# A layer's output weights taken early into the place of a finished scan, one vector's matrix moved into the up loop, and two projections of a scan in another order

## The chip, the cores and the metric

The kernel runs on one core of a Trainium2 chip. The metric is the device time of one execution in microseconds (us). TensorE (PE in the profile) multiplies matrices into PSUM, VectorE (DVE) and ScalarE (ACT) work elementwise, GpSimd (POOL) helps VectorE, and SyncE (SP) issues all the weight transfers, one queue in order. Each engine runs its own instructions strictly in the order in which they stand in its program, so an instruction that waits holds up everything behind it on that engine.

## The reference

A two-layer network over 256 context tokens and 256 latent tokens (512 columns in all, width 1024), and then a second block. The part that the change touches is layer 0 (`even_mixer`, then `conv_ffn`) and the beginning of layer 1 (`odd_mixer`, the SSD scan):

```python
mod_l = silu(c) @ mod_w[layer] + mod_b[layer]      # six vectors per layer: (layer, 0..5)
hl = modulate(xl, norm_mix_g[layer], sh1l, sc1l)
# layer 0: a GLA scan (4 heads) and an mLSTM scan (4 heads) of projections of h
yc, yl = even_mixer(hc, hl, ...)                   # concat([gla, mlstm]) @ w_out
xl = xl + g1l * yl                                 # vector 2
hl = modulate(xl, norm_ffn_g[layer], sh2l, sc2l)   # vectors 3 and 4
xl = xl + g2l * conv_ffn(hl, ...)                  # vector 5: needed after the down product only
# layer 1: SSD; each of 4 groups projects x, B, C and the gate z from h
```

## The kernel before

Every fp32 weight block is loaded into a staging tile `st` (three of them, pool `wst`), split by ScalarE into a half-precision high part `whi` and by VectorE or GpSimd into a low part `wlo`, and used in three TensorE passes; `get_w` does the load and the split, and its `parts` names the pool of the two parts. A staging tile is free for the next load when its `wlo` has been made.

The order of the instructions on each engine is set by a scheduler that builds the program, from the order in the code and from which tiles are free. A pool that is closed gives its memory to pools opened later, and a tile in that memory waits until the old tiles there have had their last reader.

Layer 0's mixer (`layer0_mixer`) goes in these steps. First `gla`: the projections of q, k, v (`gqk`, `gv`), and then four units (`gla_unit`: two pairs of heads, two streams). A unit makes eight levels of tiles `R` (VectorE subtracts, ScalarE takes the exponential, VectorE multiplies; four buffers), small products of them on TensorE (`PA`, `PB`, `fine`), picks blocks of these by masks into `acc` and `PT` (VectorE), then the output product `o`, a norm (`hsq`, `hss`, `rsqrt`, `on`) and a transpose `yT`, which ScalarE copies to `yf`. Then `mlstm_inputs`: the projections `mqk` (8 blocks of 128 rows, 512 columns), `mv`, `mo` and `gg`, 14 weight blocks of 1 MB in layer 0 in all. Then `mlstm`: four heads, each with masks `plain` and `msk`, exponentials `W`, products `S` and `nd` and a normalised sum `hm`. Last the output projection `eo` with the four weight blocks `even_o`: blocks 0 and 1 need the GLA half only, 2 and 3 the mLSTM half. Its results are added to the residual stream `xT`, which is loaded again from memory at this point. The modulation vectors are made by `mod_steps`: (0,2), (0,3), (0,4) as whole fp32 products beside the mLSTM heads, (0,5) after the output projection; those of layer 1 in half-precision halves of 0.5 MB, one in each of the 22 rounds of the FFN's up loop and the rest in the down loop. In the code all of `mlstm_inputs` comes after `gla`, and the scheduler weaves the two together.

In the SSD (`ssd`), `inputs` projects for a group x (`sx`), B and C (`sB`, `sC`) and the gate (`sz`); `steps` computes the decay terms of all groups while group 0 is projected.

Of the kernel before, what the change touches and what calls it, by code (L numbers as in the profile page):

```python
# [248 lines left out]
class Program:  # L249
# [287 lines left out]

    def layer0_mixer(self):
        h, I = self.h, self.I
        with ExitStack() as ph:  # L540
            gp = self.pool("gp", 1, None, ph)
            ev = self.pool("ev", 1, None, ph)
            mp = self.pool("mp", 1, None, ph)
            yf = ev.tile([128, 8, 512], F32, name="yf")
            mqk = ev.tile([128, 8, 512], F32, name="mqk")
            vext = ev.tile([128, 4, 4, 129], F32, name="vext")
            self.rows = [mp.tile([128, 512], F32, name=n) for n in ("li", "lf", "lb", "lm")]
            for t in self.rows:
                self.G.memset(t[:64], 0.0)
            self.G.memset(vext[:, :, :, 128:129], 1.0)  # L550
            self.gla(gp, h, I["even_w"], yf)
            self.mlstm_inputs(h, I["even_w"], mqk, vext, yf)
            for i in range(4):
                self.split(h[0][:, i], h[1][:, i], yf[:, i])
            self.mlstm(mp, h, mqk, vext, yf)
            self.dbg("ym", h[0])
        self.res2 = self.pool("res2")
        self.xT = self.res2.tile([128, 8, 512], F32, name="xT")
        self.nc.sync.dma_start(self.xT, I["xT"].rearrange("p (k t) -> p k t", k=8))
        with ExitStack() as tail:  # L560
            tw = self.pool("tw", 2, None, tail)
            w = [self.get_w(I["even_o"][b], 4, 512) for b in range(2)]
            for r in (2, 3, 4):
                for _ in self.mod_steps(0, r, whole=True):
                    pass
            w += [self.get_w(I["even_o"][b], 4, 512, parts=tw) for b in (2, 3)]

            for b in range(2):
                for c in range(4):
                    ps = self.mm("eo")  # L570
                    self.proj_fm(ps, w[b], c * 128, 128, h, 0, 512, nk=4)
                    self.add_residual(ps, 0, 2, 4 * b + c, BOTH)

            for s in range(2):
                for b in range(2):
                    for c2 in range(2):
                        ps = self.mm("eo")
                        for c in range(2):
                            self.proj_fm(ps[:, c * 256:c * 256 + 256], w[2 + b], (2 * c2 + c) * 128, 128, h,
                                         256 * s, 256 * s + 256, nk=4, h0=4)  # L580
                        for c in range(2):
                            self.add_residual(ps[:, c * 256:], 0, 2, 4 * b + 2 * c2 + c, ((s, 0, 256),), 256 * s)
                if s == 0:
                    self.norm_stream(0, 1, 0, "ml")
            for _ in self.mod_steps(0, 5, pool=tw, whole=True):
                pass
        self.dbg("xmid0", self.xT)

    def conv3(self, u, ps, w, b, streams=((0, 256), (256, 512))):
# [383 lines left out]
    def ffn(self, l, streams):  # L973
        I, V = self.I, self.V
        both = len(streams) == 2
# [4 lines left out]
        if both:  # L980
# [3 lines left out]
            for i in range(3):  # L984
                w = self.get_w(I["w_up"][l, i], 8, 256, self.G)
# [21 lines left out]
        with ExitStack() as ph:  # L1007
            fp = self.pool("fp", 1, None, ph)
            f2 = self.pool("f2", 3, None, ph)
            stage = self.pool("stage", 1 if both else 3, None, ph)  # L1010
            fcw = fp.tile([128, 44, 9], F32, name="fcw")
            self.nc.sync.dma_start(fcw, I["fcw"][l].rearrange("p (c j) -> p c j", c=44))
            hid = self.pair(fp, "hid", [128, 22, n])
            if both:
                ms, mp = self.pool("ms", 3, None, ph), self.pool("mp", 3, None, ph)
                up = True
                mods = chain.from_iterable(self.mod_steps(1, r, eng=lambda: self.G if up else None, pool=ms, parts=mp,
                                                          halves=True) for r in range(6))
            for i in range(22):
                begun = both and i < 3  # L1020
                if begun:
                    w, pss = first[i]
                elif not both and i < 2:
                    w = self.first_up[i]
                else:
                    w = self.get_w(I["w_up"][l, i], 8, 256, self.G if both or i > 2 else None, (None, stage)[i % 2])
                us = []
                for c in range(2):
                    ps = pss[c] if begun else self.mm("up")
                    a = 256 if begun else 0  # L1030
                    self.proj_fm(ps[:, a:n], w, c * 128, 128, h, a, n)
                    u = f2.tile([128, n], F32, tag=f"u{c}", name="u")
                    conv(u, ps, 22 * c + i)
                    us.append(u)
                sg = f2.tile([128, n], F32, tag="sg", name="sg")
                self.act(sg[:, :n], us[1][:, :n], AF.Silu)
                self.tt(sg[:, :n], sg[:, :n], us[0][:, :n], ALU.mult, eng=self.G)
                self.split(hid[0][:, i], hid[1][:, i], sg[:, :n], eng=self.G)
                if both:
                    next(mods)  # L1040

            def down(k, ws, a, b):
                ps = self.mm("dn")
                for j, w in enumerate(ws):
                    self.proj_fm(ps[:, a:b], w, 0, 128, hid, a, b, nk=11, h0=11 * j, first=j == 0, last=j == 1)
                    for _ in range(3 - j if both else 0):
                        next(mods, None)
                return ps

            def weights(k, j, parts=None):  # L1050
                return self.get_w(I["w_dn"][l, 2 * k + j], 11, 128, self.G if not both and k < 2 else None, (None, stage)[j], parts)

            up = False
            if not both:
                self.ahead()
            for k in range(6 if both else 8):
                self.add_residual(down(k, [weights(k, j) for j in range(2)], 0, n), l, 5, k, streams, t0)
                if not both:
                    self.before_norm(k)
                    if k >= 4 and k < 4 + 3:  # L1060
                        for i in (0, 1):
                            self.first_mg.append(self.get_w(I["w2_m"][2 * (k - 4) + i], 8, 128, self.G, stage, self.nx, 2048, 1024))
            if both:

                ws = [[weights(k, j, fp if (k, j) == (7, 1) else None) for j in range(2)] for k in (6, 7)]
                for s, a, b in streams:
                    for k in (6, 7):
                        ps = down(k, ws[k - 6], a, b)
                        self.add_residual(ps[:, a:b], l, 5, k, ((s, 0, 256),), a)
                    if s == 0:  # L1070
                        self.norm_stream(1, 0, 0)
# [15 lines left out]
    def ssd(self, sp, s2, h, y):  # L1087
        T, V, I = self.T, self.V, self.I
# [107 lines left out]
        for b in range(2):  # L1196
            w = self.get_w(sw[b], 8, 256)
# [5 lines left out]
        def inputs(g, d):  # L1203
# [3 lines left out]
            for b in range(2):  # L1207
                if g:
                    w = self.get_w(sw[5 * g + b], 8, 256)
                else:  # L1210
                    w, pss = first[b]
# [12 lines left out]
                    yield  # L1224
            if g == 0:
                d["steps"] = steps(pd)
            w = self.get_w(sw[5 * g + 2], 8, 256)
            ps = self.mm("sB")
            self.proj_fm(ps, w, 0, 128, h, 0, 512)
# [15 lines left out]
            cb = d["cb"] = s2.tile([128, 2, 128], F32, tag="cb", name="cb")  # L1245
            self.act(cb, ps[:, :256].rearrange("p (a b) -> p a b", a=2))
            yield
            sz = d["sz"] = s2.tile([128, 4, 256], F32, tag="sz", name="sz")
            for b in range(2):
                w = self.get_w(sw[5 * g + 3 + b], 8, 256)  # L1250
# [115 lines left out]

        D = {}
        take(inputs(0, D), 99)
        states(0, D)
        for g in range(4):  # L1370
# [631 lines left out]
```

## Time and profile before

| | us |
|---|---|
| median of 3 runs (1649.72 to 1652.54) | 1651.38 |
| the profiled execution, its own time | 1646.42 |
| span of the profile, first to last instruction | 1644.6 |
| TensorE busy | 1563.6 |
| VectorE busy | 1212.3 |
| ScalarE busy | 847.9 |
| GpSimd busy | 444.8 |

The profile is of one execution; its own time is 1.8 us more than its span and 5 us less than the median. Times in the rows are microseconds from the start of the span. A busy share of 95% for TensorE says that in most stretches it is TensorE's queue that sets the pace; the stretches in which it isn't busy show where another engine or a transfer does.

### The profile page before, as it was taken

The numbers are of one execution on the slowest core, as the hardware profiler recorded it, in microseconds if no ns is written. First come the engines' busy times: TensorE is split into PE (matmuls) and PEld (weight loads), VectorE is DVE, ScalarE is ACT, GpSimd is POOL, SyncE is SP. The second block draws the span as 40 slices with busy tenths as digits, with TensorE's granted clock in tenths as the row PEclk, the third lists the DMA queues.
The fourth block names the chain that finished last, engine by engine and source line by source line (L and its number), as shares of the span: only waits on it lengthen the run. The fifth ranks groups of instructions, "written<-read, shape, count | busy, mean of one in ns | idle before, by whom it ended". The sixth has DMA issues, their size and how long they took to land.

```text
span 1644.6 us, 31809 instructions
## 1 busy us (share of the span) xinstructions
PE 1563.6 (95%) x12978; PEld 1083.6 (66%) x12978; DVE 1212.3 (74%) x2637; ACT 847.9 (52%) x1390; POOL 444.8 (27%) x264
## 2 busy tenths in 40 slices
PE   6999999889999999998999999699998999999998
PEld 3565875467444444475566667488887887778877
DVE  6888856777877796557878898799977885366734
ACT  4746434334555445435555665356564644566542
POOL 0000000224878740000000000259934312431250
PEclk9999999989999999999999999799999999999999
DMA  9222135752444437532222343335454343433651
GB/s 392 89 103 79 54 126 208 258 183 80 157 149 146 138 122 254 177 120 77 103 78 95 112 141 125 124 121 199 137 194 166 141 167 111 146 116 125 228 168 52
DMA packets 41187, 236.77 MB, mean 144 GB/s; under 512 B 4689, under 2 KB 5457, under 8 KB 21201
## 3 DMA queue, kind: packets, MB, share of 16 engines
q1 hardware_dynamic: 41040, 234.74, 40.6%
q8 instruction: 102, 1.67, 0.4%
q14 instruction: 45, 0.36, 0.1%
HBM read 233.68 MB, written 1.05 MB: 143 GB/s over the span
## 4 chain that ended last, share of the span: by engine, by line
PE 81%; DVE 8%; ACT 4%; DMA 3%; issue 3%; POOL 1%; ACTq 0%; SPq 0%; DVEq 0%; POOLq 0%
PE up L332 19%; PE dn L332 9%; PE sx L332 5%; PE fm L332 4%; PE mg L332 4%; PE br L332 3%; PE mqk L332 2%; PE tm L339 2%; ACT whi L306 2%; PE so L332 2%; DVE wlo L294 2%; PE mod L505 2%; PE sz L332 2%; DVE u L303 2%; PE sc L1664 2%
## 5 line engine op out<-in xcount | busy, mean ns | idle before, releaser
L332 PEld LDWEIGHTS <-whi 128*128 128x128 f16 (+2 forms) x5240 | 511.5, 99 | 253.3 <-issue 38.1
L294 POOL TENSOR_TENSOR wlo<-st,whi 128x2048 bf16<-128x2048 f32 (+2 forms) x101 | 311.7, 3097 | 935.5 <-ACT whi L306 934.8
L306 ACT ACTIVATE whi<-st 128x2048 f16<-128x2048 f32 (+3 forms) x242 | 369.1, 1536 | 253.3 <-PE dn L332 46.6
L332 PEld LDWEIGHTS <-wlo 128*128 128x128 bf16 (+2 forms) x2620 | 258.9, 99 | 127.4 <-issue 13.6
L294 DVE TENSOR_TENSOR wlo<-st,whi 128x2048 bf16<-128x2048 f32 (+4 forms) x141 | 279.0, 1988 | 83.8 <-ACT whi L306 82.1
L303 DVE SCALAR_TENSOR_TENSOR u<-up,fcw,u 128x189 f32<-128x189 f32 (+3 forms) x792 | 297.3, 431 | 49.4 <-ACT u L306 41.5
L332 PE MATMUL up<-hh,whi 128*128 128x256 f16 (+1 forms) x752 | 238.2, 319 | 4.4 <-ACT hh L306 4.1
L332 PE MATMUL up<-hl,whi 128*128 128x256 bf16 (+1 forms) x752 | 238.1, 317 | 2.0 <-DVE hl L303 1.9
L332 PE MATMUL up<-hh,wlo 128*128 128x256 f16 (+1 forms) x752 | 237.7, 317 | 0.0
L332 PE MATMUL dn<-hidh,wlo 128*128 128x256 f16 (+1 forms) x396 | 122.2, 310 | 2.3 <-DVE wlo L294 2.3
L332 PE MATMUL dn<-hidh,whi 128*128 128x256 f16 (+1 forms) x396 | 122.3, 311 | 1.8 <-ACT whi L306 1.8
L332 PE MATMUL dn<-hidl,whi 128*128 128x256 bf16 (+1 forms) x396 | 122.5, 310 | 0.0
L306 ACT ACTIVATE u<-up,ppt,fcw 128x512 f32<-128x512 f32 (+1 forms) x88 | 58.1, 660 | 47.9 <-PE up L332 47.9
L332 PE MATMUL fm<-hh,whi 128*128 128x256 f16 x288 | 78.5, 273 | 0.5 <-DVE xc L303 0.5
L332 PE MATMUL fm<-hh,wlo 128*128 128x256 f16 x288 | 78.6, 273 | 0.0
L332 PE MATMUL fm<-hl,whi 128*128 128x256 bf16 x288 | 78.5, 273 | 0.0
L332 PE MATMUL mg<-hh,wlo 128*128 128x256 f16 x256 | 71.0, 277 | 3.6 <-POOL wlo L294 3.6
L332 PE MATMUL mg<-hl,whi 128*128 128x256 bf16 x256 | 71.0, 278 | 1.2 <-DVE hl L303 1.2
L332 PE MATMUL mg<-hh,whi 128*128 128x256 f16 x256 | 70.7, 277 | 0.9 <-ACT mgt L306 0.9
L339 PEld LDWEIGHTS <-hh 128*128 128x128 f16 x640 | 61.5, 99 | 8.8 <-issue 1.1
L298 POOL TENSOR_SCALAR E<-E,rs 128x128 f32<-128x128 f32 (+1 forms) x48 | 37.1, 786 | 107.3 <-DVE rs L1675 47.9
L294 POOL TENSOR_TENSOR sg<-sg,u 128x512 f32<-128x512 f32 (+1 forms) x44 | 44.2, 1004 | 45.6 <-ACT sg L306 45.3
(539 smaller groups left out, 3050.8 us busy)
## 6 DMA issues: line engine op xcount, KB each, us to landing
st<-in_w_up_dram SPq DMA_DIRECT2D x44, 1024.0 KB, 4.8
st<-in_w_dram SPq DMA_DIRECT2D x25, 1024.0 KB, 4.9
st<-in_mod_w_dram SPq DMA_DIRECT2D x48, 512.0 KB, 4.7
st<-in_w_dn_dram SPq DMA_DIRECT2D x32, 704.0 KB, 4.1
st<-in_ssd_w_dram SPq DMA_DIRECT2D x20, 1024.0 KB, 4.9
st<-in_mod_w_dram SPq DMA_DIRECT2D x16, 1024.0 KB, 6.4
st<-in_w_m_dram SPq DMA_DIRECT2D x32, 512.0 KB, 4.3
st<-in_even_w_dram SPq DMA_DIRECT2D x14, 1024.0 KB, 5.0
```

The lines of the kernel that those rows point to most:

```text
L294: (eng or self.V).tensor_tensor(o, a, b, op=op)
L298: (eng or self.V).tensor_scalar(o, a, s1, None, op0=op0)
L303: self.V.scalar_tensor_tensor(o, a, s, b, op0=op0, op1=op1)
L306: self.S.activation(o, i, func, **kw)
L332: self.T.matmul(ps, w[a][:, k, c0:c0 + cw], h[b][:, h0 + k, t0:t1], start=first and k == 0 and i == 0, stop=last and k == nk - 1 and i == 2)
L339: self.T.matmul(ps, h[b][:, k, t0:t0 + 128], w[a][:, k, c0:c0 + cw], start=k == 0 and i == 0, stop=k == nk - 1 and i == 2)
L505: T.matmul(ps[32 * j:32 * j + 32, :256], c[:, 2 * b + k], w[:, 0 if halves else k, 256 * j:256 * j + 256], start=b == k == i == 0, stop=b ...
L1664: T.matmul(ps[:, a:b], q[r, tb * 128:tb * 128 + 128], k[r, 0:b - a], start=True, stop=False)
```

## The change

Four edits. The GLA tiles (`gp`) go to the right side of the memory and are closed when `gla` ends, and the four `even_o` blocks are fetched and split at that point, ahead of the mLSTM projections, their low parts on GpSimd and their parts in the place of the GLA tiles (`tw`, four buffers). The vector (0,5) is no longer made after the output projection, but in halves at the head of the chain that the up loop draws from, two halves in each of the first 8 rounds. The residual stream's tile is still opened after the mixer's left-hand pools are closed. In the SSD, group 0's gate projections come ahead of its B and C.

```diff
     def layer0_mixer(self):
         h, I = self.h, self.I
+        tail = self.ctx.enter_context(ExitStack())
         with ExitStack() as ph:
-            gp = self.pool("gp", 1, None, ph)
+            gs = ExitStack()
+            gp = self.pool("gp", 1, None, gs, side="right")
...
             self.gla(gp, h, I["even_w"], yf)
+
+            gs.close()
+            tw = self.pool("tw", 4, None, tail, side="right")
+            w = [self.get_w(I["even_o"][b], 4, 512, self.G, parts=tw) for b in range(4)]
             self.mlstm_inputs(h, I["even_w"], mqk, vext, yf)
...
-        with ExitStack() as tail:
-            tw = self.pool("tw", 2, None, tail)
-            w = [self.get_w(I["even_o"][b], 4, 512) for b in range(2)]
+        with tail:
             for r in (2, 3, 4):
...
-            w += [self.get_w(I["even_o"][b], 4, 512, parts=tw) for b in (2, 3)]
...
-            for _ in self.mod_steps(0, 5, pool=tw, whole=True):
-                pass
...
-                mods = chain.from_iterable(self.mod_steps(1, r, eng=lambda: self.G if up else None, pool=ms, parts=mp,
-                                                          halves=True) for r in range(6))
+                mods = chain.from_iterable(self.mod_steps(*m, eng=lambda: self.G if up else None, pool=ms, parts=mp,
+                                                          halves=True) for m in ((0, 5), *((1, r) for r in range(6))))
...
-                if both:
+                for _ in range(0 if not both else 2 if i < 8 else 1):
                     next(mods)
...
             if g == 0:
                 d["steps"] = steps(pd)
+                yield from gate(g, d)
...
+            if g:
+                yield from gate(g, d)
```

The change moves far more instructions than it edits. TensorE's program of the kernel before, where the GLA units begin: behind the first small products (`PA`, `fine`, `PB`) stand already the matmuls of `mqk`, the first mLSTM projection, and they alternate with GLA products from here on.

```order
L736 MATMUL PA<-R 128x256 x8
L802 MATMUL fine<-QK 32x32 x13
L780 MATMUL PB<-R 128x128 x2
L780 MATMUL PB<-R 64x64 x4
L802 MATMUL fine<-QK 32x32 x3
L332 LDWEIGHTS whi
L332 MATMUL mqk<-hh,whi 128x512
L332 LDWEIGHTS whi
L332 MATMUL mqk<-hl,whi 128x512
```

TensorE's program of the changed kernel, where the first `mqk` matmul stands now: right behind the last unit's `o` and `yT`.

```order
L832 MATMUL o<-gv,PC 128x128 x2
L838 MATMUL yT<-ept,on 128x128 x4
L332 LDWEIGHTS whi
L332 MATMUL mqk<-hh,whi 128x512
L332 LDWEIGHTS whi
L332 MATMUL mqk<-hl,whi 128x512
```

All products of the four GLA units stand ahead of the first projection of the mLSTM; before, only those of the first rows above did. Between the units there are only the masks `plain` and `msk` of three of the mLSTM's eight head directions.

ScalarE's program of the changed kernel at the same place (`yf` is the copy of a unit's output, `whi` a high part, `u` the evacuation of a projection):

```order
L306 ACTIVATE hsq<-o 128x512
L306 ACTIVATE yf<-yT,hglag 128x256 x2
L306 ACTIVATE whi<-st 128x2048 x7
L306 ACTIVATE u<-mqk,hcb,hcw 128x512
```

The seven high parts, four of `even_o` and then three of `mqk`, stand behind the last unit's copy; before, the high parts of the projections stood between the units' exponentials.

SyncE's queue before, from the small GLA load `a` on:

```order
L625 DMA a_517<-in_a_dram 128x512
L315 DMA st<-in_even_w_dram 128x2048 x9
L315 DMA st<-in_even_o_dram 128x2048 x2
L315 DMA st<-in_mod_w_dram 128x2048 x2
L559 DMA xT<-in_xT_dram 128x4096
L315 DMA st<-in_mod_w_dram 128x2048 x10
L315 DMA st<-in_even_o_dram 128x2048 x2
L315 DMA st<-in_w_up_dram 128x2048 x2
```

And in the changed kernel:

```order
L626 DMA a_517<-in_a_dram 128x512
L315 DMA st<-in_even_o_dram 128x2048 x4
L315 DMA st<-in_even_w_dram 128x2048 x10
L315 DMA st<-in_mod_w_dram 128x2048 x12
L315 DMA st<-in_w_up_dram 128x2048 x6
L565 DMA xT<-in_xT_dram 128x4096
L1013 DMA fcw<-in_fcw_dram 128x396
```

The four `even_o` loads have moved ahead of ten `even_w` loads, through the same three staging tiles, and the load of `xT` has moved from behind two modulation loads to behind all twelve and six loads of the up weights; it waits there for VectorE, where before it waited for TensorE. The rounds of the up loop from the ninth on, the down loop, layer 1's FFN and the second block have the same order in both kernels.

## Rows read from the trace of the kernel before

**Rows 1.** The page: busy time, share of the span, instructions.

```profile
PE 1563.6 (95%) x12978; PEld 1083.6 (66%) x12978; DVE 1212.3 (74%) x2637; ACT 847.9 (52%) x1390; POOL 444.8 (27%) x264
```

**Rows 2.** Windows: stretch, length, busy time of each engine, clock, DMA share, GB/s.

```profile
90.60:251.70 161.10, 157.42 (x2493) 107.71 (x2492) 123.01 (x342) 80.39 (x165) 0.00 (x0) 1.00 0.24 86
251.70:312.10 60.40, 60.40 (x458) 36.33 (x458) 38.51 (x143) 25.45 (x77) 4.07 (x1) 1.00 0.59 216
312.10:354.20 42.10, 35.71 (x259) 25.20 (x258) 33.85 (x67) 16.61 (x23) 16.35 (x5) 0.96 0.73 266
354.20:366.70 12.50, 7.54 (x74) 3.93 (x74) 9.32 (x27) 5.34 (x13) 0.00 (x0) 0.73 0.50 185
```

**Rows 3.** Windows: the GLA units, from their first `R` to the last `on`.

```profile
94.80:231.50 136.70, 133.02 (x2344) 94.11 (x2341) 108.39 (x315) 69.47 (x145) 0.00 (x0) 1.00 0.19 65
```

**Rows 4.** VectorE's groups by form, 93.6 to 232: count, busy, mean ns, idle before.

```profile
L294 DVE TENSOR_TENSOR wlo<-st,whi 128x2048 bf16<-128x2048 f32 x9 | 20.6, 2291 | 8.2 <-ACT whi L306 7.7 <-PE o L831 0.6
L809 DVE COPY_PREDICATED acc<-lvl,fine 128x64 f32<-128x64 uint32 x72 | 15.6, 224 | 11.1 <-PE fine L802 5.3 <-ACT acc L306 5.1
L303 DVE SCALAR_TENSOR_TENSOR u<-mqk,hcw,u 128x510 f32<-128x510 f32 x16 | 11.9, 742 | 0.2
...
L303 DVE SCALAR_TENSOR_TENSOR mqk<-th,u 128x512 f32<-128x512 f32 x8 | 5.5, 690 | 1.9 <-ACT th L306 1.8
```

**Rows 5.** The chain of waits: GLA's `gv`, its first product, one block of `gg`.

```profile
69.56 21.12 PE gv L339 x192
90.68 2.89 PE PA L736 x16
...
246.48 5.18 PE gg L332 x24
```

**Rows 6.** A window of 5 us in which the granted clock is 0.50.

```profile
780.00:785.00 5.00, 2.54 (x12) 1.82 (x13) 5.00 (x11) 2.98 (x6) 0.00 (x0) 0.50 0.59 206
```

**Rows 7.** Groups by form: ScalarE's high part (69 to 225), GpSimd's low parts (span).

```profile
L306 ACT ACTIVATE whi<-st 128x2048 f16<-128x2048 f32 x10 | 19.1, 1906 | 9.5 <-PE gv L339 4.7 <-PE mqk L332 4.2 <-PE mo L339 0.6
L294 POOL TENSOR_TENSOR wlo<-st,whi 128x2048 bf16<-128x2048 f32 x43 | 177.2, 4121 | 803.8 <-ACT whi L306 803.8
L294 POOL TENSOR_TENSOR wlo<-st,whi 128x1024 bf16<-128x1024 f32 x54 | 124.1, 2300 | 130.6 <-ACT whi L306 129.9 <-PE br L332 0.6
L294 POOL TENSOR_TENSOR hidl<-sg,hidh 128x512 bf16<-128x512 f32 x22 | 28.4, 1292 | 12.8 <-ACT hidh L306 7.7 <-PE mod L505 4.4 <-PE up L332 0.7
```

**Rows 8.** Transfers: queue, count, KB each, median us from issue to landing.

```profile
st<-in_even_w_dram SPq DMA_DIRECT2D x14, 1024.0 KB, 5.0
xT<-in_xT_dram SPq DMA_DIRECT2D x1, 2048.0 KB, 9.6
```

**Rows 9.** VectorE in order of time: the gated head sums, first and last of four.

```profile
261.88 0.69 DVE L303 SCALAR_TENSOR_TENSOR hm<-yf,hm 128x512 f32<-128x512 f32 x1
...
312.12 0.69 DVE L303 SCALAR_TENSOR_TENSOR hm<-yf,hm 128x512 f32<-128x512 f32 x1
```

**Rows 10.** The chain of waits from the output projection to the up loop.

```profile
347.56 6.14 PE eo L332 x56
...
356.16 6.79 DMA st<-in_mod_w_dram
...
366.74 4.87 PE up L332 x29
```

**Rows 11.** In order of time: a GpSimd low part, and a VectorE instruction beside it.

```profile
318.95 5.62 POOL L294 TENSOR_TENSOR wlo<-st,whi 128x2048 bf16<-128x2048 f32 x1 [9.33 <-ACT whi L306]
320.57 4.02 DVE L303 SCALAR_TENSOR_TENSOR r<-rt,r 128x4 f32<-128x4 f32 x1
```

**Rows 12.** The chain of waits in the up loop, one round.

```profile
411.99 0.33 PE mod L505 x8
412.32 10.47 PE up L332 x48
```

**Rows 13.** Windows: the start of the SSD.

```profile
760.00:800.00 40.00, 30.77 (x228) 22.63 (x226) 37.50 (x63) 27.16 (x37) 0.00 (x0) 0.91 0.35 119
```

More of the change, by code (lines that the diff above doesn't have):

```diff
@@ L1247, in inputs, with gate @@
             yield
+            if g:
+                yield from gate(g, d)
+        def gate(g, d):
             sz = d["sz"] = s2.tile([128, 4, 256], F32, tag="sz", name="sz")
```

## The prediction

> **What bounds the kernel now.** I read the page first. TensorE is busy for 95% of the span [rows 1], so a change pays only if it takes work off TensorE or fills one of its gaps, and it costs whatever it adds to those gaps. The windows come next, to find the gaps around the edited code [rows 2]. From GLA's first products to the last `gg` (90.6 to 251.7) TensorE is busy 157.4 of 161.1 at full clock. Those 161.1 hold two things: the GLA units and 104 us of mLSTM projections. One `mqk` or `gg` block is 24 matmuls in 5.18, and the 192 matmuls of a `v` projection take 21.1 [rows 5], so 8 x 5.18 + 4 x 5.18 + 2 x 21.1 = 104.4. Within the units alone (94.8 to 231.5) VectorE is busy 108.4 of 136.7 and ScalarE 69.5 [rows 3], so the units are held by a chain through VectorE and ScalarE, and the projections fill TensorE meanwhile. The heads then take 60.4 with TensorE full, the output projection 42.1 with 35.7 busy, and the wait for vector (0,5) 12.5 with 7.5 busy and a clock of 0.73 [rows 2].
>
> **What decides the change.** The program orders of the two kernels are above. In the changed one all GLA products precede the first `mqk` matmul. An in-order TensorE then cannot run a projection during GLA, and the cover that [rows 2] shows is gone. The reason lies in the staging tiles: the four `even_o` loads come first, their parts lie in the memory of the GLA tiles, and so no staging tile is released to `even_w` before GLA ends.
>
> **1. GLA alone.** VectorE's own work for the units is 108.4 less what belongs to the projections [rows 3, 4]: 8 of the low parts (8 x 2.29 = 18.3), `u` 11.9, `mqk` 5.5. That leaves 72.7. It is the floor if no chain stalled. The ceiling at full clock keeps every idle microsecond: 136.7 - 35.7 = 101. TensorE's own products there are some 53 (157.4 - 104.4) and are thinly spread. A window in which TensorE is busy 2.5 of 5 had a granted clock of 0.50 [rows 6], the lower of the two levels; at that level 53 becomes 106, and I let a third of the added 53 lie on the chain, which is 16 to 18 us. I take 72.7 + 14 (half of VectorE's 28.3 idle) + 16 = 103, with bounds 73 and 101 + 16 = 117. GLA starts at 90.68 + 2.89 = 93.6 [rows 5], so it ends with the copy `yf` near 198.
>
> **2. The handover.** Behind the last copy ScalarE begins the high parts. The first three staging tiles hold `even_o`. The first is released after a high part of 1.9 and a GpSimd low part of 4.1 [rows 7]; the fourth `even_o` block follows into it, and the first `mqk` block takes the second tile, released one low part later. Its load takes 5.0 [rows 8], then 1.9 for its high part and 2.3 for the low part on VectorE [rows 4]. 1.9 + 2 x 4.1 + 5.0 + 1.9 + 2.3 = 19.3; I take 17 to 24. TensorE has nothing else in its queue then. The projections begin near 217.4.
>
> **3. The projections alone.** 104.4, about 4 of first mLSTM products, and 3.5 for a start at the lower clock: 111.8, so the last `gg` ends near 329 where it ended at 251.7. Terms 1 to 3 together are **+77.6**.
>
> **4. From the last `gg` to the up loop.** Before: 60.4 + 42.1 + 12.5 = 115 [rows 2]. The 60.4 held 49 `eo` matmuls, about 10.6 at 5.18 / 24 each; the new order has 24 there (5.2), because a third pair of PSUM banks would wait for `xT`. The chain of a head stays: the gated sums stand (312.1 - 261.9) / 3 = 16.7 apart [rows 9]. I take 57. The load of `xT` has moved past ten more modulation loads and six `w_up` loads on SyncE's queue, and past its old place: it now lies where `yf` was, and waits for the last gated sum of the heads. Each load that is ahead of it on SyncE is done by then, and `fcw` behind it is needed only in the FFN. It takes 9.6 [rows 8] and about 0.9 to be seen, and no residual can be added before it. Behind it come 72 `eo` matmuls of 0.216 (15.5) and 192 of 6.14 / 56 = 0.11 [rows 10] (20.9), with 3.5 for the start at the lower clock. 57 + 9.6 + 0.9 + 15.5 + 20.9 + 3.5 = 107.4. Gone are the wait of 6.8 for the last `mod_w` block and the `mod` products behind it [rows 10]. This is **-7.8** (bounds -18, if the `eo` half that doesn't wait fills more, and +3, if the norms between the streams keep their stalls of 42.1 - 35.7). The up loop also no longer starts out of a stretch with a granted clock of 0.73 [rows 2], but behind full `eo` work: **-2**.
>
> **5. The up loop.** Eight more halves cost TensorE 8 x 0.33 = 2.7. A round lasts 0.33 + 10.47 [rows 12], about 11.1 with the small gaps that I allow it. GpSimd's work in one of the first eight rounds rises by a 0.5 MB low part from 4.12 + 2.30 + 1.29 and a product like the last, 9.0, to 11.3 [rows 7]: as long as the round. I add 2 for stalls: **+5** (2.7 to 14, where 14 is 8 rounds that each stretch by 1.4 beyond the products).
>
> **6. The SSD.** From 760 to 800 TensorE is idle 9.2 of 40, and in one part the clock is 0.50 [rows 6, 13]. Group 0's gate products now stand ahead of B and C and can fill a part of this; but the decay steps, for which VectorE is busy 37.5 of 40, end no earlier. **-4** (-9 to +4, the last if B and C come late for the scan).
>
> **The sum.** +77.6 - 7.8 - 2 + 5 - 4 = **+69**. The profiled execution took 1646.4, which gives 1715; it lies 5 below the median of the runs, so the median comes to 1651.4 + 69, **1720**.
>
> **One thing that the rows show of a shared port.** A VectorE instruction `r` on four columns took 4.02 from 320.57, while a GpSimd low part ran from 318.95 to 324.57 [rows 11]; `r` ended when GpSimd did, and one on 512 columns takes 0.69 [rows 4]. The Trainium skill ("SBUF — State Buffer", section "Who interferes with whom") says that a VectorE instruction with two inputs in SBUF and a GpSimd instruction reading SBUF share a port pair as an exclusive lock and that the second is blocked in full. By that rule `r` waited for GpSimd, and the trace agrees with its 4.02. Three low parts of `w_up` blocks now fall among the mLSTM heads, whose chain has many such VectorE instructions; by that rule the heads could lose up to 3 x 4.1 = 12 us as an estimate and the sum would be +81. The sum goes without it, since those parts may fall into VectorE's waits.
>
> **The rivals.**
>
> *GLA alone runs near VectorE's pace.* If the trace's idle of 28.3 is mostly waiting for TensorE behind projections, GLA alone takes about 80 (72.7 and a quarter of the idle). For it: VectorE's largest idle before `acc` is put down to TensorE's `fine` [rows 4], which queued behind projections. Against it: ScalarE shares the chain. Then 69 - 23 = +46, **1697**.
>
> *The lower clock throughout, and GpSimd as the bound of the up loop.* GLA at its ceiling of 117 (+14), the handover at 24 (+5), the up loop at 14 (+9), the heads with GpSimd's low parts (+8): +105, **1756**. For it: [rows 6, 11].
>
> *The output stage doesn't shorten.* The code fetches `even_o` early so that nothing waits for it, but `eo`'s results need `xT`, which comes late; if the norms keep all their stalls and the heads their 60.4, term 4 is +8 instead of -7.8: +85, **1736**.
>
> *The other side: not slower.* VectorE's durations in [rows 4] might be lengthened by the engines and transfers that work beside it. Without projections GLA would then be short. With every other term kept, 103 - 69 = 34 is the length of GLA alone at which the change costs nothing; if its instructions took 0.4 of their time, 72.7 becomes 29 and the total **1646**. Against it: the means in [rows 4] go with the size, 224 ns for 64 columns and 742 for 510, which waits for others would blur.
>
> **How the numbers follow.** The sum as forecast, with GLA alone between 90 and 117: 0.60. Near VectorE's pace: 0.18. Lower clock and GpSimd: 0.14. No shorter output stage: 0.05. Not slower: 0.03. The range leaves out the last and the far half of the third, and a part of the second where the other terms are at their lower bounds: 1684 to 1754. About 0.2% is what a measurement of this kernel can tell from no change, 3.3 us; with every term of the sum at its lower bound and GLA at 73 (-30, -2, -10, -2, -5 from +69) the change still costs 20, so slower has 0.96, and the rest is split.
>
> **What would show it.** Right: a stretch of some 100 us from 93.6 on with TensorE busy about half and a granted clock below 1, and no `mqk` before the last `yT`; a gap of near 19 before the first `mqk`; the projections in some 110 with TensorE full; the `xT` load after the last head and `eo` idle before it; no wait for `mod_w` ahead of the up loop, and its first eight rounds longer than the ninth; less idle time at the start of the SSD. Wrong: GLA's end before 165 (the first rival), a GLA stretch beyond 120 or rounds of 12.5 (the second), or `eo` that ends more than 115 behind the last `gg` (the third).

## The result, and the profile after

The changed kernel takes 1757.64 us (median of 4 runs, 1750.79 to 1759.32) against 1651.96 of the kernel before: 1.0639 times as long, 95% interval 1.0606 to 1.0673. The direction was forecast; the time lies 38 above the forecast of 1720 and 4 beyond its range. The profiled execution took 1757.39, its span 1755.6; before they were 1646.42 and 1644.6, so the spans differ by 111.0.

The windows of the changed kernel by its stages (stretch, length, busy time of PE, PEld, DVE, ACT and POOL, clock, DMA share, GB/s) stand against [rows 2, 3]:

```profile
93.97:208.00 114.03, 71.51 (x1786) 55.70 (x1788) 76.35 (x282) 43.86 (x120) 0.00 (x0) 0.57 0.01 2
208.00:226.76 18.76, 1.67 (x3) 0.43 (x4) 3.27 (x1) 9.15 (x6) 16.12 (x4) 0.50 0.55 179
226.76:336.24 109.48, 108.46 (x677) 68.03 (x683) 47.03 (x52) 34.31 (x39) 0.00 (x0) 0.99 0.30 104
336.24:405.85 69.61, 55.55 (x436) 35.16 (x438) 46.97 (x146) 30.11 (x84) 12.16 (x3) 0.93 0.62 227
405.85:454.89 49.04, 40.42 (x270) 27.83 (x273) 23.17 (x67) 6.07 (x14) 0.00 (x0) 0.86 0.13 48
454.89:473.81 18.92, 7.79 (x46) 5.53 (x46) 16.16 (x36) 7.98 (x16) 6.65 (x3) 0.73 0.63 222
```

They are GLA alone, the handover, the mLSTM projections alone, the heads, the output projection, and the norm of the second stream. In the first VectorE is busy 76 of 114 and TensorE's granted clock is 0.57; in the third TensorE is full, doing what had been hidden in [rows 3]. The heads, full in [rows 2], now leave TensorE idle for 14, and the transfers in the first stretch move 2 GB/s: the staging tiles are held.

The chain of waits of the changed kernel (start, length, what), at the handover, in the heads and around the output projection:

```profile
212.47 4.06 POOL wlo L294
216.54 4.92 DMA st<-in_even_w_dram
221.49 1.92 ACT whi L306
223.43 3.29 DVE wlo L294
226.76 10.83 PE mqk L332 x43
...
377.25 2.65 DVE den L294
...
382.35 1.80 ACT whi L306
...
384.24 4.07 DVE den L294
...
388.54 3.78 DVE den L298
...
405.85 8.48 DMA xT<-in_xT_dram
...
416.09 13.24 PE eo L332 x50
429.38 19.00 PE eo L332 x154
...
454.89 3.81 DMA st<-in_mod_w_dram
...
460.60 1.74 DVE hl L303
462.35 2.26 DVE sq L294
...
465.00 1.88 DVE hl L303
```

The first five lines are the handover as it was forecast: a low part on GpSimd, the load, the two parts, the first products. The three `den` work on two columns each. In order of time GpSimd stands beside them, and beside the norm:

```profile
375.79 4.08 POOL L294 TENSOR_TENSOR wlo<-st,whi 128x2048 bf16<-128x2048 f32 x1 [151.23 <-ACT whi L306]
384.22 8.07 POOL L294 TENSOR_TENSOR wlo<-st,whi 128x2048 bf16<-128x2048 f32 x2 [4.35 <-ACT den L306]
459.94 6.65 POOL L294 TENSOR_TENSOR wlo<-st,whi 128x1024 bf16<-128x1024 f32 x3 [67.65 <-ACT whi L306]
```

Each `den` lasts until a GpSimd low part ends, as `r` did in [rows 11]. The chain also has a `mod_w` load (3.81) in it, though the forecast had the wait for `mod_w` gone. It is the first half of (0,5), and SyncE issued it only behind the last `eo` matmul, as its list of waits says (total, times, longest):

```profile
SPq L315 <- PE eo L332: 48.2, 1, 48.2
```

For the experiments the program is cut at a few instructions, by the first and last start of a tile's instructions: GLA from the first `PA` to the last `on`; projections from `PA` to the last `gg`; heads from there to the last gated sum `hm`; output to the last `eo`; norm to the first `up` matmul; up loop to the first `dn`; SSD from the first `sx` to the last `so`. The down loop is 127.0 to 127.1 in all. Each row is one trace.

| kernel | GLA | PA to gg | heads | output | norm | up loop | SSD |
|---|---|---|---|---|---|---|---|
| before | 140.2 | 160.7 | 60.8 | 41.9 | 12.6 | 240.7 | 316.7 |
| changed | 113.2 | 245.0 | 69.0 | 50.0 | 10.5 | 247.1 | 322.0 |
| only_even_o | 112.7 | 244.9 | 56.7 | 49.5 | 23.1 | 245.4 | 321.0 |
| only_mod | 140.0 | 160.5 | 67.2 | 36.0 | 6.2 | 245.8 | 319.3 |
| only_ssd | 141.0 | 161.5 | 60.9 | 42.5 | 12.5 | 241.2 | 320.6 |
| fetch_late | 137.3 | 158.6 | 72.7 | 50.5 | 10.8 | 247.1 | 315.6 |
| early2 | 141.2 | 162.5 | 72.5 | 49.2 | 10.6 | 247.1 | 319.3 |
| early3 | 113.4 | 242.2 | 68.3 | 49.1 | 10.6 | 246.9 | 319.3 |
| up_held | 113.6 | 245.9 | 58.0 | 50.5 | 10.6 | 247.1 | 322.2 |
| xt_on_yf | 140.0 | 160.5 | 65.0 | 48.8 | 13.0 | 241.9 | 313.9 |
| late_dve | 140.2 | 161.5 | 68.0 | 49.6 | 8.0 | 247.8 | 322.7 |
| no_ssd | 113.8 | 246.1 | 68.1 | 50.6 | 10.7 | 247.1 | 316.8 |
| repaired | 137.4 | 158.7 | 62.9 | 50.1 | 10.8 | 247.1 | 318.5 |

From before to changed: 84.8 more up to the last `gg` (336.1 against 251.3), 20.6 from there to the first `dn` (376.6 against 356.0), 5.3 in the SSD, 0.3 elsewhere: 111.0.

### The profile page after: what moved, and what is told of

Its sections match the earlier page's. It is cut to its first block, busy times and chain, and to the rows that moved or that the text cites. A ratio compares the mean times of both kernels' runs of the same rounds, so it can differ in the third digit from the quotient of the medians.

```text
span 1755.6 us, 31800 instructions
## 1 busy us (share of the span) xinstructions
PE 1593.4 (91%) x12914; PEld 1104.1 (63%) x12978; DVE 1217.4 (69%) x2633; ACT 856.3 (49%) x1398; POOL 475.3 (27%) x276
## 4 chain that ended last, share of the span: by engine, by line
PE 76%; DVE 12%; ACT 4%; DMA 4%; issue 3%; POOL 1%; ACTq 0%; SPq 0%; another core or an unknown queue 0%; DVEq 0%; POOLq 0%
PE up L332 18%; PE dn L332 9%; PE sx L332 4%; PE fm L332 4%; PE mg L332 3%; PE eo L332 2%; PE br L332 2%; PE tm L339 2%; DVE wlo L294 2%; ACT whi L306 2%; PE sz L332 2%; PE mqk L332 2%; PE so L332 2%; DVE u L303 2%; PE sc L1670 1%
## 5 line engine op out<-in xcount | busy, mean ns | idle before, releaser
L294 POOL TENSOR_TENSOR wlo<-st,whi 128x2048 bf16<-128x2048 f32 (+2 forms) x113 | 343.4, 3052 | 1024.0 <-ACT whi L306 1019.4
L306 ACT ACTIVATE whi<-st 128x2048 f16<-128x2048 f32 (+3 forms) x250 | 377.4, 1522 | 281.6 <-PE up L332 51.3
L294 DVE TENSOR_TENSOR wlo<-st,whi 128x2048 bf16<-128x2048 f32 (+4 forms) x137 | 274.7, 2017 | 122.7 <-ACT whi L306 121.9
L332 PE MATMUL up<-hl,whi 128*128 128x256 bf16 (+1 forms) x733 | 231.2, 316 | 1.6 <-DVE hl L303 1.5
L332 PE MATMUL dn<-hidl,whi 128*128 128x256 bf16 (+1 forms) x384 | 117.2, 306 | 0.0
L298 POOL TENSOR_SCALAR E<-E,rs 128x128 f32<-128x128 f32 (+1 forms) x48 | 37.0, 783 | 111.8 <-DVE rs L1681 51.1
L332 PE MATMUL sx<-hh,whi 128*128 128x512 f16 (+1 forms) x160 | 54.2, 345 | 4.6 <-DVE u L303 4.6
```

Of the source, the lines that this page charges most:

```text
L294: (eng or self.V).tensor_tensor(o, a, b, op=op)
L298: (eng or self.V).tensor_scalar(o, a, s1, None, op0=op0)
L306: self.S.activation(o, i, func, **kw)
L332: self.T.matmul(ps, w[a][:, k, c0:c0 + cw], h[b][:, h0 + k, t0:t1], start=first and k == 0 and i == 0, stop=last and k == nk - 1 and i == 2)
```

## The experiments

**The three edits one by one.** `only_even_o` has the GLA pool on the right, the early fetch and the late `xT`; `only_mod` the move of the vector (0,5); `only_ssd` the last. Each is cut out of the diff above; `only_even_o` keeps this behind the output projection:

```diff
+            for _ in self.mod_steps(0, 5, whole=True):
+                pass
```

> Only the first edit: GLA tiles on the right, even_o fetched and split at GLA's end, xT loaded late; vector (0,5) whole after the output projection and the SSD as in the kernel before. Theory (the early fetch is nearly all of the loss): last gg near 336 as in the changed kernel (+84), up loop 15 to 25 later still, so 1745 to 1760. Rival (the loss behind the last gg comes from the vector (0,5) and the SSD edits): +84 and no more, near 1735 or below.

> Only the second edit: vector (0,5) in halves, two in each of the first eight rounds of the up loop. The prediction's step (the wait of 6.8 for the last block goes, +5 in the up loop, -2 for the clock): near 1648. Rival (that wait stood beside the norm of the second stream, which needs the 13 us anyway, and the halves' GpSimd low parts now block VectorE in that norm): no gain or a loss, 1652 to 1658.

> Only the third edit: group 0's gate blocks ahead of its B and C. The prediction's step: -4, near 1647. Rival (as the changed kernel's trace has it, where the SSD from its first sx to its last so is 5.3 longer): near 1657.

Measured on one chip, where the kernel before took 1646.70: `only_even_o` 1750.19, ratio 1.0614 (1.0586 to 1.0643); `only_mod` 1647.68, 0.9987 (0.9966 to 1.0008); `only_ssd` 1653.27, 1.0033 (1.0012 to 1.0054). The first edit is nearly the whole loss; with it alone no low part of `w_up` stands among the heads, and they take 56.7. The second gives nothing that can be told from noise, though the -3.8 of the prediction's terms for it lies within the interval too (-5.6 to +1.3; the terms are -6.8, +5 and -2). What became of the wait of [rows 10] is seen in the scale `rbc` of the kernel before, and in the chain of waits of `only_mod`:

```profile
371.61 0.43 PE rbc L375 x2
```

```profile
355.54 0.47 DVE nt L303
356.01 0.79 DVE xT L303 x2
...
359.38 0.40 DVE hl L303
359.77 0.35 DVE sq L294
360.12 0.14 issue
360.25 0.98 PE ssq L367 x4
361.24 6.31 PE up L332 x35
367.55 0.43 PE rbc L375 x2
```

No transfer is left there, but VectorE's norm of the second stream is. The up loop begins 5.5 earlier, so the wait was worth about that, but `rbc` comes only 4.1 earlier, and from its first matmul to the first `dn` the up loop takes 5.1 more (245.8 against 240.7): 1.4 up to `rbc`, 3.6 behind it, where the eight halves are.

**Why the projections left GLA.** `fetch_late` moves the two lines of the fetch behind the projections:

```diff
             gs.close()
+            self.mlstm_inputs(h, I["even_w"], mqk, vext, yf)
             tw = self.pool("tw", 4, None, tail, side="right")
             w = [self.get_w(I["even_o"][b], 4, 512, self.G, parts=tw) for b in range(4)]
-            self.mlstm_inputs(h, I["even_w"], mqk, vext, yf)
```

> The changed kernel with the four even_o fetches moved behind the mLSTM projections in the code; GLA on the right, the parts in its place, late xT, (0,5) in halves and the SSD order stay. Theory (it is the order of the loads through the three staging tiles that takes the projections out of GLA): last gg back near 252, the rest of the loss (some 20 behind the last gg, 5 in the SSD) stays, 1670 to 1685. Rival (the GLA tiles' place or the late release of their memory holds up the projections in any order): last gg near 330, 1740 or more.

It took 1671.56, ratio 1.0131 (1.0096 to 1.0165), and from `PA` to the last `gg` it needs 158.6 again: most of the loss is the place of the fetch in the code. `early2` and `early3` leave two or three blocks early (`range(2)` or `range(3)` there, the rest behind the projections).

> The changed kernel with only two of the four even_o blocks fetched at GLA's end, the other two behind the mLSTM projections: one staging tile is left to the projections during GLA. Theory (the projections are out of GLA because all three staging tiles are held): the projections run beside GLA again, one block per round of load 5.0, high part 1.9, low part 2.3 of that one tile, 1665 to 1705. Rival (any even_o load ahead of them holds the projections): 1745 or more.

> The same with three of the four blocks fetched at GLA's end: all three staging tiles are held, and the fourth block is no longer ahead of the projections. Theory (a step at three tiles): no mqk before the last yT, 1740 to 1758. Rival (the cost grows with each block fetched early): about a third of the way back, 1715 to 1735.

They took 1673.66 (ratio 1.016, 1.0121 to 1.02) and 1748.19 (1.0613, 1.0567 to 1.0659). The first and last start of the first projection's matmuls, in `early2` and then in `early3`, and in `early3` VectorE's `on`:

```profile
L332 PE MATMUL mqk<-hh,whi x64: 379/379/634, 99.2 to 158.4; 128*128 128x512 f16 x64
```

```profile
L332 PE MATMUL mqk<-hh,whi x64: 379/379/634, 218.2 to 266.3; 128*128 128x512 f16 x64
L294 DVE TENSOR_TENSOR on<-o,r x4: 691/691/692, 125.9 to 202.7; 128x512 f32<-128x512 f32 x4
```

It is a step, not a slope. With one staging tile left the projections run beside GLA as before, at no cost that the time shows; with the third block all tiles are held and the first `mqk` comes behind the last `on`.

**GLA alone and the clock.** `fill` and `fill3` add six and three 512-column matmuls per GLA level, which nobody reads:

```diff
         def level(B):
+            ps = self.ps("mm", "fill")
+            for i in range(6):
+                T.matmul(ps, self.h[0][:, i % 8, 0:128], self.h[0][:, i % 8], start=True, stop=True)
```

> The changed kernel with six 512-column matmuls per GLA level added that nobody reads (work that isn't the reference's; the result is unchanged). Theory (in GLA alone TensorE's own small products run at the lower clock and lie on the chain): the granted clock in that stretch goes from 0.57 to 0.9 or more and the stretch of 114 shrinks by 8 to 18, total 1738 to 1750. Rival (the chain is VectorE's and ScalarE's, the clock doesn't matter): within 4 of the changed kernel, or longer, where the added matmuls stand in front of the products.

> The changed kernel with three instead of six unread 512-column matmuls per GLA level. Theory (the lower clock lies on GLA's chain, and six of them stood in the way of GLA's own products): clock above 0.8 in GLA and the stretch to the last on shorter than the changed kernel's 111 by 5 to 12. Rival (the clock doesn't matter to the chain): 108 to 116.

`fill` took 1757.66 (ratio 1.067, 1.0625 to 1.0716), with the first `PA` to the last `on` at 119.1 and a clock of 1.00 up to 174: what the clock may have given, the added matmuls in TensorE's queue (192 of them, at 0.216 each 41) took again. `fill3` took 1753.40 (ratio 1.0644, 1.0601 to 1.0688), with that stretch at 108.0, where the other six traces with GLA alone and nothing added have 112.5 to 113.8. (The expectation counts from behind the first products to the end of the last `on`, 111 in the changed kernel; by that cut `fill3` has about 106, at the end of the theory's range.) Its windows:

```profile
93.60:205.00 111.40, 78.68 (x1883) 54.70 (x1884) 75.96 (x282) 46.31 (x122) 1.66 (x1) 0.81 0.01 3
94.00:114.00 20.00, 19.43 (x524) 11.36 (x523) 17.20 (x60) 12.05 (x36) 0.00 (x0) 1.00 0.01 3
114.00:134.00 20.00, 19.48 (x321) 10.20 (x320) 11.26 (x41) 10.35 (x30) 0.00 (x0) 1.00 0.01 2
134.00:154.00 20.00, 13.12 (x258) 10.23 (x257) 17.52 (x66) 8.20 (x21) 0.00 (x0) 0.95 0.01 2
154.00:174.00 20.00, 12.14 (x424) 10.43 (x425) 16.02 (x58) 6.92 (x20) 0.00 (x0) 0.50 0.01 3
```

By the starts of the four `on`, the first two units are 2.9 and 0.8 shorter than in the changed kernel, the third, at 0.50 in both, is as long (25.8), and the fourth 1.5 shorter. So the lower clock lies on GLA's chain with some 5, by this one trace, in which VectorE's order is also slightly another. How much of the forecast 16 it is stays open, since the clock fell again in the second half; the total shows no gain.

**The heads.** `up_held` gives the first three `w_up` blocks staging tiles over `mqk` and `vext`, which come free when the heads end:

```diff
+            hold = ExitStack()
+            us = self.pool("us", 3, None, hold)
             for i in range(3):
-                w = self.get_w(I["w_up"][l, i], 8, 256, self.G)
+                w = self.get_w(I["w_up"][l, i], 8, 256, self.G, us)
```

> The changed kernel with staging tiles of their own for the first three w_up blocks, in the memory where mqk and vext were, so that none of their high and low parts stands among the mLSTM heads. Theory (the heads take 69 instead of the forecast 57 because six splits of w_up stand in ScalarE's, VectorE's and GpSimd's programs beside them): heads 57 to 61, total 8 to 12 below the changed kernel, if the splits hide beside eo. Rival (the heads are long for another reason, or the splits now delay the up loop by as much): within 4 of the changed kernel.

> The changed kernel once more, as the yardstick for the other three on the same chip: 1752 to 1760.

`up_held` took 1748.42, the changed kernel on the same chip 1761.73, 2 above what was expected of it (ratios 1.0605, 1.0569 to 1.0641, and 1.0685, 1.0659 to 1.0711). That is 13 less, a little more than the theory had. The windows of `up_held` of the heads and of the output projection:

```profile
335.20:393.20 58.00, 53.36 (x436) 34.39 (x438) 36.15 (x146) 24.55 (x81) 0.00 (x0) 1.00 0.58 219
393.20:443.70 50.50, 40.94 (x272) 27.92 (x274) 23.99 (x69) 11.87 (x17) 12.13 (x3) 0.86 0.27 109
```

GpSimd's three low parts (12.13) now stand beside `eo`, the heads take 58.0, and the output projection is hardly longer for it (50.5 for 50.0). One of the last `den` in its chain of waits:

```profile
389.33 0.17 DVE den L294
```

None of its `den` takes longer than 0.17, where three in the changed kernel's chain take 2.65, 4.07 and 3.78. That is 10.0 more, of the 11 by which the heads differ. Up to the first of these three the `den` of both kernels keep a distance of 0.7 to 0.9. What it is worth to move the low parts is what `late_dve` asks, which has `fetch_late`'s first three `w_up` blocks and first three halves split on VectorE:

```diff
-                w = self.get_w(I["w_up"][l, i], 8, 256, self.G)
+                w = self.get_w(I["w_up"][l, i], 8, 256)
...
+                up, lead = True, iter([None] * 3)
-                mods = chain.from_iterable(self.mod_steps(*m, eng=lambda: self.G if up else None, pool=ms, parts=mp,
+                mods = chain.from_iterable(self.mod_steps(*m, eng=lambda: next(lead, self.G) if up else None, pool=ms, parts=mp,
```

> The kernel with the fetch behind the projections (1671.6), with the low parts of the first three w_up blocks and of the first three halves of (0,5) on VectorE instead of GpSimd. Theory (GpSimd's low parts block VectorE's two-input instructions in the heads and in the norm: den 3.2 and 3.4, hl 1.7 and 1.9, sq 2.3): 6 to 10 less, 1661 to 1666. Rival (those instructions are late for another reason, and VectorE now has six low parts more on its queue): no gain, 1668 to 1676.

It took 1668.72 (1.0143, 1.0107 to 1.0179): no `den` takes longer than 0.17, but three low parts of 2.28 stand on VectorE among the heads, which are 4.7 shorter than `fetch_late`'s 72.7; the total can't be told from that kernel's (1.0131). The same edit on other kernels, `before_dve` (its first line alone, on the kernel before) and `mod_dve` (all of it, on `only_mod`):

> The kernel before, with the low parts of the first three w_up blocks on VectorE. Theory (the r of 4.02 on the chain of waits behind the heads is VectorE blocked by GpSimd): 2 to 5 faster, 1642 to 1645. Rival (VectorE's own 3 x 2.3 takes the place of the stall): no change, 1645 to 1649.

> The kernel with the second edit alone (vector (0,5) in halves in the up loop, 1647.7), with the low parts of the first three w_up blocks and of the first three halves on VectorE. Theory (the 3 to 4 that the removed wait gave was lost to blocked VectorE instructions, sq 2.0 and 2.2, v 1.9, r 4.0): 1639 to 1644, faster than the kernel before. Rival (what it gave was lost in the up loop, to eight more halves on GpSimd): no change, 1645 to 1650.

They took 1655.52 (1.0037, 1.0005 to 1.0069) and 1646.83 (0.9990, 0.9966 to 1.0013), beside 1648.30; neither is faster. In `before_dve` no `r` takes longer than 0.17, but VectorE has three more low parts of some 2.28, and the output stage is 4.5 longer than before. The stall of 4 is real, and moving the low parts to VectorE buys nothing.

**The late xT.** `xt_on_yf` is the kernel before with one pool more, so that `xT` lies where `yf` was; `mqk_first` is `fetch_late` with `mqk` allocated ahead of `yf`:

```diff
+            yp = self.pool("yp", 1, None, ph)
             gp = self.pool("gp", 1, None, ph)
...
-            yf = ev.tile([128, 8, 512], F32, name="yf")
+            yf = yp.tile([128, 8, 512], F32, name="yf")
```

> The kernel before with one thing altered: yf has a pool of its own, opened ahead of the GLA tiles, so that xT's tile lies where yf was and not where the GLA tiles were; GLA, the fetches of even_o, vector (0,5) and the SSD stay. The order of eo becomes that of the changed kernel (24 matmuls beside the heads, 207 behind). Theory (the late xT makes the output stage longer by 5 to 8 and the heads too, because w_up's low parts run beside them): 1654 to 1668. Rival (the prediction's step: the late load only moves eo work, and the stage gets shorter or stays): 1640 to 1649.

> The kernel with the fetch behind the projections, and mqk allocated ahead of yf, so that xT's tile lies where mqk was: its load waits for the last S product of the heads, not for the last gated sum. Theory (the late xT holds the output projection, 9.6 of load in the open): the load begins 8 to 15 earlier, eo follows the heads at once, 1671 becomes 1656 to 1664. Rival (the six w_up loads ahead of it on SyncE, or the heads' own length, hold it): no change, 1668 to 1675.

`xt_on_yf` took 1656.80 against 1648.30 (1.0076, 1.0041 to 1.0112), with this in its chain of waits:

```profile
316.57 8.61 DMA xT<-in_xT_dram
...
328.23 11.29 PE eo L332 x50
339.57 18.35 PE eo L332 x151
```

The late load makes heads and output projection 4.2 and 6.9 longer. `mqk_first` took 1670.18 (1.0139, 1.0105 to 1.0173), no change: its load is issued at 318.5, still behind the `w_up` loads, and lands before VectorE, whose program has the additions to `xT` behind the last head's norm, comes to them at 330.7. Giving back the memory alone didn't move an instruction that already stood late.

**The SSD.** `no_ssd` is the changed kernel with the old order of the gate.

> The changed kernel with the SSD's order of before. Theory (the third edit costs about 5, as its run alone had it): 4 to 6 below the changed kernel of the same call. Rival (the edit fills one gap and opens others of the same size, and the 5 came from elsewhere): within 2.

`no_ssd` took 1749.87 (1.0623, 1.0596 to 1.0649), the changed kernel on the same chip 1761.73 (1.0685, 1.0659 to 1.0711): the edit makes the kernel slower in both comparisons, by 0.0033 of the time (5.4) in its own run and by 0.0062 (10) here, where the two intervals don't meet and the theory had 4 to 6. The windows from 25.6 behind the first `sx` on, of `no_ssd` and then of the changed kernel:

```profile
864.60:904.60 40.00, 31.02 (x228) 22.97 (x228) 37.72 (x65) 25.84 (x35) 0.00 (x0) 0.91 0.34 114
904.60:944.60 40.00, 39.79 (x216) 21.51 (x218) 29.60 (x48) 26.95 (x58) 0.00 (x0) 1.00 0.26 88
944.60:997.10 52.50, 52.29 (x344) 33.16 (x346) 42.92 (x85) 31.23 (x66) 0.00 (x0) 1.00 0.25 88
```

```profile
865.40:905.40 40.00, 32.58 (x233) 23.08 (x234) 38.15 (x59) 25.60 (x34) 0.00 (x0) 0.96 0.45 158
905.40:945.40 40.00, 39.46 (x213) 21.37 (x214) 25.47 (x44) 24.30 (x49) 0.00 (x0) 0.96 0.16 53
945.40:999.70 54.30, 50.62 (x328) 31.32 (x332) 44.00 (x90) 31.41 (x71) 0.00 (x0) 1.00 0.23 78
```

The gate fills 1.6 of the early gap (idle 7.4 instead of 9.0), and 3.8 more stand idle later (0.5 and 3.7 instead of 0.2 and 0.2). The first `sB` starts 44.7 behind the first `sx` instead of 33.0. The size isn't settled beyond that: with the old order the SSD takes 313.9 to 321.0 in the table, with the new one 315.6 to 322.7.

**Together.** `repaired` is the changed kernel with the edits of `fetch_late`, `up_held` and `no_ssd`.

> The changed kernel with three causes taken away together: even_o fetched behind the projections, the first three w_up blocks held in staging tiles over mqk and vext, and the SSD's order of before. What stays is the late xT and vector (0,5) in halves. Theory (the parts add: 1757.6 less 84 for the projections, less 11 for the heads, less 5 to 10 for the SSD): 1650 to 1660, above the kernel before by the late xT. Rival (the parts overlap, and with the projections back beside GLA the held w_up gains nothing): 1662 to 1668.

It took 1664.44 against 1649.77 (1.0090, 1.0068 to 1.0113): the parts overlap, as the rival had it. Its reason isn't borne out: against `fetch_late` the heads go from 72.7 to 62.9, so the held `w_up` does gain there. But `xT` (8.32 in its chain of waits), an output stage of 50.1 and a `mod_w` load of 4.12 behind it stay. No kernel here beats the kernel before by more than the measurement can tell.

## Why the prediction was off, step by step

- **GLA alone, handover, projections** (forecast 103, 19.3, 111.8, in sum +77.6). Measured 111 (93.97 to the end of the last `on` at 205), 20.2 (206.6 to 226.8) and 109.3; +84.8. Mechanism right, shown by `fetch_late` and by the step from `early2` to `early3`; GLA was 8 too short. My share of a third for the clock and a half for the idle time was a guess between 73 and 117; `fill3` shows some 5 of the 16 that I put down to the clock. The two terms of 3.5 for a start at the lower clock came from no row. In the changed kernel's trace the granted clock is 0.50 from 226 to 228, 0.61 to 230 and 1.00 behind that, and 0.50 from 416 to 420, 0.82 to 422 and 1.00 behind that; what this costs, counted from the first product, is an estimate of 1.4 and 2.3.
- **From the last `gg` to the up loop** (forecast 107.4, -7.8, and -2 for the clock; 107.4 less 115 is -7.6). This is the step that failed: 129.5 instead of 107.4. Of the 22, the heads are 12.0 (69.0 for 57) and the stretch from the last `eo` to the first `up` 10.5, for which the sum had nothing; the `xT` load and the `eo` work behind it, forecast 50.4, took 50.0.
- **The heads in that step.** I had seen that three low parts of `w_up` come among them, put their price at up to 12, and left it out of the sum since they might fall into VectorE's waits. They didn't: three `den` of the chain were held up by 10.0 in all, and with the splits held back the heads take 58.0 (`up_held`). The first edit alone doesn't bring the low parts there: with the loads of (0,5) still ahead of `w_up` the heads take 56.7 (`only_even_o`), as forecast.
- **The norm in that step.** I took the 12.5 of [rows 2] for the wait for `mod_w` [rows 10] and let all of it go. The norm of the second stream runs beside that wait, and 6.2 is left where the wait is gone (`only_mod`). In the changed kernel the halves come to stand there instead: SyncE issues their loads from 454.89 on, behind the last `eo`, where `only_mod` has them at 324.77. Their high parts stand in ScalarE's program between the instructions of the norm, which leaves VectorE idle for 1.0, and their low parts on GpSimd stand beside `hl`, `sq` and `hl`, which take 1.74, 2.26 and 1.88 where `only_mod` has about 0.4 each. That is read off the traces; no run tests it alone.
- **Up loop** (+5, bounds 2.7 to 14). `only_mod` has +5.1, of which 1.4 is the start that waits for `rbc`.
- **SSD** (-4, bounds -9 to +4). Wrong sign: +5.3 in the trace, slower in both timed comparisons. The gap filled by 1.6, less than forecast, and B and C came 11.7 later, the case for which the prediction had +4.
- **The sum** missed by 42 in the spans: 7.2 in GLA and projections, 25.4 from `gg` to `dn` (+20.6 for -4.8), 9.3 in the SSD, 0.3 elsewhere.
- **The rivals.** The lower clock with GpSimd as the bound came nearest in time (1756). One of its terms was right, the heads with GpSimd's low parts (+8; measured +12); the others were not: GLA stayed within 117, the handover within 24, and the up loop at +5. So its time was near by luck. The rival at 1736, an output stage that doesn't shorten, named the right place, and its sign came: `eo` ended 119 behind the last `gg`. I gave it 0.05, and +8 where the stage took +14.2; the two terms that it names (6.4 of stalls and 3.4 of heads) give +2 and not +8.
- **The shared port.** That GpSimd blocks VectorE, as the Trainium skill has it ("SBUF — State Buffer", section "Who interferes with whom"), agrees with the 2.65 and 4.07 of `den`, which have two inputs; the 3.78 is of an instruction with one tensor input, to which the rule as I quoted it doesn't apply. The price of up to 12 was near: these three lost 10.0. It is not what can be won by moving the low parts to VectorE, where their own time takes the place of a part of it (4.7 in `late_dve`).

## What to carry to other kernels

A prefetch whose destination isn't free doesn't wait alone: it holds a staging tile, and when the last tile is held, everything behind it in the queue leaves the stage that was hiding it. Count the staging tiles against the blocks fetched early; here two of three cost nothing, the third 75. When a wait is removed, list what ran beside it, since that is what the stage costs next, and look where the tile of the load that replaces it lies, since its work can come to stand at the same place. When a load moves, move the work that its data brings along in the same sum, and price it unless a row shows that it falls into a wait.

## What was not expected of the hardware

Traces differ before the edited code is reached: the first `PA` starts between 89.3 and 95.6, with a granted clock of 0.66 to 1.00 in the ten us from 60 on. A difference of 5 between two profiles is worth nothing until it is placed; the 7.8 by which the span of `only_ssd` is longer is 5.0 ahead of its first `PA`.
